# A hybrid decoder step on one core: the first norm's small products cut into pieces, operand differences emitted earlier, the first conv pair ordered by ready k, single PSUM banks placed first

## Chip, cores and metric

The kernel runs on one core of one Trainium2 chip. The metric is the device time of one execution in microseconds; where several executions were timed, the median stands. TensorE multiplies matrices into PSUM, VectorE and ScalarE do elementwise work and read PSUM, GpSimd does small copies, some sums and accumulating loads, and SyncE issues most loads.

## The reference, cut

One decoder layer works on 512 prompt tokens and 64 sample tokens with 1024 channels, in float32.

```python
xn = rms_norm(h, g_mix[i])
z = xn @ w_in[i]                       # 1024 x 6144: b, c, hc, v, two gates
ya, cb = gated_short_conv(b, c, hc, conv_bufs[i], w_conv[i])   # b * conv3(c * hc)
ya = ya @ w_out_conv[i]
yb, pb = multiscale_pool(v, pool_bufs[i], pos0, w_pool[i], pool_scale[i])
h = h + (gate_a * ya + gate_b * yb) @ w_o[i]
hn = rms_norm(h, g_mlp[i])
h = h + jnp.square(jax.nn.relu(hn @ w_up[i])) @ w_down[i]      # 1024 -> 4096 -> 1024
gp = jax.nn.sigmoid(rms_norm(h, g_ple[i]) @ w_ple_gate[i])
h = h + gp * (p[i] @ w_ple_proj[i])
return rms_norm(h, g_final), ...
```

## The kernel before

Channels lie on the 128 partitions, in NJ = 8 tiles; the 576 tokens lie on the free axis as NH = 2 halves of HT = 288 columns. Every float32 product is made of three products of a reduced type: each operand is split into `hi` (a cast on ScalarE, line 93 or 96) and `lo` (the remainder, on VectorE, line 94 or 97), and `mm` (line 104) issues hi x hi, hi x lo, lo x hi. A unit of 128 output channels over 8 k tiles and two halves is 48 such products; `product` (line 118) issues one. The input is scaled by the gain alone; the factor `r` of the norm is applied to the results.

Weights come through one stream (lines 180 to 247) in the order in which they are used. A load goes into one of eight raw slots, a split into one of seven slots (NF = 7); `take` splits ahead as far as these slots go, and with `live` it counts units that are still held. SyncE's queue issues the loads, GpSimd's queue those that add a second weight block to a loaded one.

Some matrix products are done as a two by two block scheme with seven block products (`pairs_of`, line 416). Its operands are blocks of the activations and differences of blocks: `Operand.differences` (line 407) makes three subtractions for each of four k pairs (lines 409, 411, 412) into a tile `gt` from a tile `gx`, and splits the four results, which are called `t1`, `t3` and `t2`, `t4`. The tiles `gx`, `gt` and the later `g` share two buffers under the tag "g". In `pairs_of`, `quarter` issues the 12 products of one block (four k pairs of three). With `late`, which before is set only for the first MLP block, the first four quarters leave their last k pair to the end, and five weights are held at once.

The opening runs so. The squares of the input are summed (`Rms.add`). Three first units (c, h and b of channel tile 0, in six single PSUM banks `ps0`) run over k in the outer loop (lines 486 to 488), 18 products for each k. After k = 5 `Rms.tokens` issues the norm's sums: 36 matmul instructions as the trace counts them, each with one moving column, followed by a root on ScalarE (line 333) and a chain of five small steps on VectorE that ends in `y` (line 340). After k = 6 `Rms.spread` brings `y` to all partitions (line 347), and `copies` makes `r` and its square `rs`. Then come channel tiles 0 and 4 of the conv branch (lines 554 to 569): the multiply of c by `rs` (line 558), the product with h, the convolution (line 526), the gate (line 538, first read of PSUM at line 542), and behind these the differences of two k pairs each. From line 571 on, three pairs of conv tiles and then the gates run through `pairs_of`.

Two things set the order. A planner takes the instructions in the order in which the program emits them, as priorities, and places on each engine the first one that it reckons to be ready by its own times; so an instruction can stand earlier than its line. From line 570 on (`pinned`), and again in the MLP, TensorE's products keep the program's order. Each engine then executes its own list in order.

PSUM has eight banks. The opening has one tile of two banks and six single ones, the middle part (lines 622 to 697) four tiles of two banks, the part from line 706 again one tile of two banks, allocated first, and six single ones (lines 707, 708), and the end four tiles of two. A new part's tile waits for the readers of the tiles that lay at its place. The middle part has 32 product tiles, which take the four places in turn; line 691 reads the last two. The part from line 706 opens with two units in four single banks (`two_products`, line 370).

Of the kernel before, what the change touches and what calls it, by code (L numbers as in the profile page):

```python
# [7 lines left out]
F32 = mybir.dt.float32  # L8
# [4 lines left out]
P = 128  # L13
D = 1024
NJ = D // P
# [3 lines left out]
NH = 2  # L19
HP = SEQ // NH  # L20
HB = DB // NH
HT = HP + HB * DS
# [12 lines left out]
G_MIX, W_CONV, P_SCALE, G_MLP, G_PLE, G_FINAL = 0, 1, 4, 5, 6, 7  # L35
NV = 8
KH = D // 2
NQ = NJ // 2
# [4 lines left out]
def tile_hybrid_step(ctx: ExitStack, tc: tile.TileContext, x, pt, vecs, rc, ident, sconv, spool, w_first, w_in,  # L43
                     w_pool, w_oc, w_o, w_up, w_down, w_pg, w_pp,
                     y_out, ncp, npp, ncs, nps):
    nc = tc.nc
# [10 lines left out]
    def pool(name, bufs, **kw):  # L57
        return scope.enter_context(tc.tile_pool(name=name, bufs=bufs, reuse_waits="tile", **kw))

    tmp, acts2 = pool("tmpx", 4), pool("acts1", 10)  # L60
    psum = pool("psumx", 1, space=bass.MemoryType.PSUM)
# [42 lines left out]
    def mm(outs, w, c, m, act, start, stop):  # L104

        wh, wl = (t[:, c % KH:c % KH + m] for t in w[c // KH])
        for i, (wt, at) in enumerate(((wh, act[0]), (wh, act[1]), (wl, act[0]))):
            for o, cols in outs:
                matmul(o, wt, cols(at), start=start and i == 0, stop=stop and i == 2)

    def both(ps):
        return [(ps[h] if isinstance(ps, list) else ps[:, h, :HT], lambda t, h=h: t[:, h, :]) for h in range(NH)]
# [5 lines left out]
    def product(unit, operands, base=0, m=P, step=P):  # L118

        ps = psum.tile([P, NH, 512], F32, tag="ps", name="ps") if banks is None else [bank() for _ in range(NH)]  # L120
        n = len(operands)
        steps(ps, unit, operands, range(n), base, m, step, 0, n - 1)
        return ps
# [129 lines left out]
    def v(i, j):  # L253
        return vec[:, i, j:j + 1]
# [47 lines left out]

    class Rms:
        def __init__(self, n=NH, width=HT, chunk=HT // 3):
            self.n, self.width, self.chunk, self.parts = n, width, chunk, []
            self.shape = [P, n, width]
            self.at = [(h, c) for h in range(n) for c in range(0, width, chunk)]

# [10 lines left out]
            else:  # L319
                nc.gpsimd.tensor_tensor(out=self.parts[0], in0=self.parts[0], in1=sq, op=ALU.add)  # L320

        def tokens(self, pin=False):

            n, m = len(self.at), self.chunk
            self.ps = ps = psum.tile([P, NH, 512], F32, tag="ps", name="psn")
            sums = ps[:m, 0, self.width:self.width + n]
            for i, (h, c) in enumerate(self.at):
                for k, a in enumerate(self.parts):
                    nc.tensor.matmul(  # L329
                        sums[:, i:i + 1], a[:, h, c:c + m], ones32[:, 0:1],  # L330
                        start=k == 0, stop=k == len(self.parts) - 1)
            rt, ms, y, t = (tmp.tile([m, n], F32, tag=g, name=g, bufs=2) for g in ("rt", "ms", "ry", "rz"))
            i = nc.scalar.activation(rt, sums, AF.Sqrt, bias=epst[:m], scale=1.0 / D)
            if pin:
                tc.keep_in_program_order(i)
            nc.vector.tensor_scalar(out=ms, in0=sums, scalar1=1.0 / D, scalar2=EPS, op0=ALU.mult, op1=ALU.add)
            nc.vector.reciprocal(y, rt)
            nc.vector.tensor_tensor(out=t, in0=y, in1=y, op=ALU.mult)
            nc.vector.scalar_tensor_tensor(out=t, in0=t, scalar=-0.5, in1=ms, op0=ALU.mult, op1=ALU.mult)
            nc.vector.scalar_tensor_tensor(out=y, in0=t, scalar=1.5, in1=y, op0=ALU.add, op1=ALU.mult)  # L340
            self.y = y

        def spread(self):

            m = self.chunk
            for i, (h, c) in enumerate(self.at):
                nc.tensor.matmul(  # L347
                    self.ps[:, h, c:c + m], self.y[:, i:i + 1].broadcast_to([m, P]), idt[:m, :m],
                    start=True, stop=True)
            return self.ps[:, :self.n, :self.width]  # L350
# [132 lines left out]
    for j in range(NJ):  # L483
        stat.add(xs[j], part=j >= NJ - 2)
    ps0 = [[bank() for _ in range(NH)] for _ in range(3)]
    for k in range(NJ):
        for u in range(3):
            mm(both(ps0[u]), [first[k]], u * P, P, xg[k], k == 0, k == NJ - 1)
        if k == 5:
            stat.tokens()  # L490
        if k == 6:
            r1, r1s = stat.copies(stat.spread(), "r", "rs")

    ncp_t = tmp.tile([P, NJ, CW - 1], F32, tag="ncp", name="ncp_t", bufs=1)
    xo = Operand(10)
# [4 lines left out]
    class Conv:  # L500
# [37 lines left out]
        def gate(self, ps):  # L538
# [11 lines left out]
                op=ALU.mult)  # L550
            ya_in[self.j] = split_act(bt)

    ya_in = [None] * NJ
    for j in (0, NQ):
        ps_c = ps0[0] if j == 0 else product(stream.take(2), xg)
        c = tmp.tile([P, NH, HT], F32, tag="t", name="c")
        for h in range(NH):
            nc.vector.tensor_tensor(out=c[:, h], in0=ps_c[h], in1=r1s[:, h], op=ALU.mult)
        ps_h = ps0[1] if j == 0 else product(stream.take(2), xg)
        conv = Conv(j)  # L560
        for h in range(NH):
            conv.half(h, ps_h[h], c[:, h])
        conv.convolve()
        conv.gate(ps0[2] if j == 0 else product(stream.take(2), xg))
        for k in range(j // 2, j // 2 + 2):
            g = tmp.tile([P, 4, HT], F32, tag="g", name="gx", bufs=2)
            for i in range(2):
                nc.scalar.mul(g[:, 2 * i:2 * i + 2], xs[k + i * NQ], v(G_MIX, k + i * NQ))
            xo.differences(k, g)
    pinned = True  # L570
    for q in range(1, NQ):

        def corner(i, g, c11):
            if i == 0:
                conv.lo = tmp.tile([P, NH, HT], F32, tag="t", name="c")
                nc.vector.tensor_tensor(out=conv.lo[:, 1], in0=c11, in1=r1s[:, 1], op=ALU.mult)
            else:
                conv.now.half(1, c11, conv.lo[:, 1])

        def finish(i, g):  # L580
            if i == 0:
                nc.vector.tensor_tensor(out=conv.lo[:, 0], in0=g[:, 0], in1=r1s[:, 0], op=ALU.mult)
                conv.hi = tmp.tile([P, NH, HT], F32, tag="t", name="c")
                nc.vector.tensor_tensor(out=conv.hi, in0=g[:, 2:4], in1=r1s, op=ALU.mult)
                conv.now = Conv(q)
            else:
                conv.now.half(0, g[:, 0], conv.lo[:, 0])
                conv.now.convolve()
                conv.then = Conv(q + NQ)
                conv.then.whole(g[:, 2:4], conv.hi)  # L590
                conv.now.gate(conv.ps)
                conv.then.convolve()

        def filler():
            conv.ps = product(stream.take(2), xg)

        pairs_of(2, xo, corner, finish, filler=filler)
        conv.then.gate(product(stream.take(2), xg))


# [103 lines left out]
    for j in halved:  # L704
        nc.sync.dma_start(xs[j], x[:, j])
    tmp = pool("tmpm", 3)
    psum = pool("psumm", 1, space=bass.MemoryType.PSUM)
    banks = pool("banks", 6, space=bass.MemoryType.PSUM)
    acts2 = pool("acts2", 6)
    pinned = True  # L710

# [215 lines left out]
```

## Time and profile before

| | |
|---|---|
| median of 3 executions | 896.02 us (894.7 to 897.62) |
| profiled execution | 897.59 us |
| its span | 895.8 us |
| mean granted clock of TensorE | 0.988 |
| busy: TensorE, VectorE, ScalarE, GpSimd | 98%, 65%, 45%, 15% of the span |

TensorE is busy nearly all the time, and a busy row does not say at which clock. The views used below are the page's summary, the list of waits, the timelines of single engines (each row is a run of like instructions: start, time from the first start to the last end, engine, line, operation, tiles, count, and in brackets the idle time before it and what ended it), and tables of stretches with the granted clock.

### The profile page before, as it was taken

Reading aid. Unit: us, or ns where it says so; the run is one execution under the profiler, and the core shown is the slowest. Engines: PE = TensorE matmul, PEld = TensorE weight load, DVE = VectorE, ACT = ScalarE, POOL = GpSimd, SP = SyncE. Lnnn points to the kernel's source line nnn. Section 1 sums busy time; section 2 is a strip of 40 time slices with the busy share of each in tenths; the row PEclk is TensorE's granted clock in tenths of the full one; section 3 lists DMA queues with packets and bytes.
Section 4 is the critical chain, followed back from the end, with each engine's and each line's share of the span. In section 5 each row is a group of like instructions: output and inputs, shape, how many; then the busy total and the mean of one; then the engine's idle time right before and its main releaser. Section 6 shows DMA issues by size and latency. Waiting matters only on the chain.

```text
span 895.8 us, 16709 instructions
## 1 busy us (share of the span) xinstructions
PE 878.8 (98%) x6554; PEld 875.5 (98%) x6554; DVE 581.2 (65%) x1027; ACT 405.0 (45%) x702; POOL 131.1 (15%) x168
## 2 busy tenths in 40 slices
PE   9989999999999999999999999999999999999995
PEld 9979999999999999999999999999999999999995
DVE  7886887985336677767884347534773367687455
ACT  7643443553113333345774237522672157536432
POOL 4101111100001221022110100011000110021354
PEclk9889999999999999999999999999999999999998
DMA  7526455554222222363553535353543544332002
GB/s 258 133 81 145 140 128 149 139 147 140 83 83 83 83 83 83 114 194 92 134 155 104 133 97 137 121 130 101 154 133 87 124 122 130 104 97 94 14 16 91
DMA packets 58125, 103.88 MB, mean 116 GB/s; under 512 B 6848, under 2 KB 10560, under 8 KB 58048
## 3 DMA queue, kind: packets, MB, share of 16 engines
q1 hardware_dynamic: 50416, 89.16, 31.0%
q0 software_dynamic: 7488, 13.63, 9.7%
q8 instruction: 51, 0.84, 0.4%
q14 instruction: 26, 0.21, 0.1%
q10 hardware_dynamic: 144, 0.03, 0.0%
HBM read 99.82 MB, written 2.99 MB: 115 GB/s over the span
## 4 chain that ended last, share of the span: by engine, by line
PE 94%; DVE 3%; DMA 1%; ACT 1%; issue 1%; SPq 0%; DVEq 0%
PE b L67 68%; PE ps L67 18%; PE psg L67 6%; DVE lo L94 1%; PE psn L329 1%; PE psn L347 1%; DMA raw<-w_up 1%; DMA xin<-x 0%; ACT hi L93 0%; DVE xall L808 0%; DVE t L691 0%; DVE gt L409 0%; ACT hi L96 0%; DVE gt L412 0%; DVE gt L411 0%
## 5 line engine op out<-in xcount | busy, mean ns | idle before, releaser
L67 PE MATMUL b<-hi 128*128 128x288 f32 x1592 | 403.1, 298 | 5.2 <-ACT hi L93 3.6
L67 PE MATMUL b<-lo,hi 128*128 128x288 f32 x1592 | 402.1, 297 | 0.7 <-DVE lo L94 0.7
L67 PE MATMUL b<-hi,lo 128*128 128x288 f32 x1592 | 402.1, 297 | 0.4 <-DVE lo L94 0.4
L93 ACT CAST hi<-raw 128x512 fp32r<-128x512 f32 x300 | 184.6, 620 | 323.6 <-PE b L67 214.6
L67 PEld LDWEIGHTS b<-hi 128*128 128x128 f32 x1592 | 278.0, 190 | 6.8 <-ACT hi L93 4.3
L94 DVE TENSOR_TENSOR lo<-raw,hi 128x512 fp32r<-128x512 f32 x300 | 210.6, 707 | 112.0 <-ACT hi L93 108.9
L67 PEld LDWEIGHTS b<-lo,hi 128*128 128x128 f32 x1592 | 278.1, 190 | 1.3 <-DVE lo L94 1.2
L67 PEld LDWEIGHTS b<-hi,lo 128*128 128x128 f32 x1592 | 277.7, 190 | 0.7 <-DVE lo L94 0.7
L67 PE MATMUL ps<-hi 128*128 128x288 f32 x416 | 89.2, 296 | 0.0
L67 PE MATMUL ps<-hi,lo 128*128 128x288 f32 x416 | 89.1, 296 | 0.0
L67 PE MATMUL ps<-lo,hi 128*128 128x288 f32 x416 | 89.1, 296 | 0.0
L154 POOL DMA_DIRECT2D raw<-w_up x32 | 27.7, 865 | 327.6 <-DMA raw<-w_up 188.8
L67 PEld LDWEIGHTS ps<-hi,lo 128*128 128x128 f32 x416 | 67.0, 189 | 0.0
L67 PEld LDWEIGHTS ps<-lo,hi 128*128 128x128 f32 x416 | 67.0, 189 | 0.0
L67 PEld LDWEIGHTS ps<-hi 128*128 128x128 f32 x416 | 67.0, 189 | 0.0
L320 POOL TENSOR_TENSOR sq<-sq 128x576 f32<-128x576 f32 (+2 forms) x32 | 41.2, 1286 | 112.3 <-ACT sq L314 64.6
L174 DVE TENSOR_TENSOR s<-raw 128x512 f32<-128x512 f32 x26 | 17.9, 690 | 49.3 <-DMA raw<-w_up 32.5
L93 ACT CAST hi<-s 128x512 fp32r<-128x512 f32 x52 | 32.0, 617 | 38.1 <-PE b L67 33.0
L94 DVE TENSOR_TENSOR lo<-s,hi 128x512 fp32r<-128x512 f32 x52 | 35.7, 687 | 13.1 <-ACT hi L93 12.1
L67 PE MATMUL psg<-hi 128*128 128x320 f32 (+1 forms) x128 | 38.2, 298 | 0.7 <-ACT r L354 0.7
L67 PE MATMUL psg<-lo,hi 128*128 128x320 f32 (+1 forms) x128 | 37.9, 296 | 0.0
L67 PE MATMUL psg<-hi,lo 128*128 128x320 f32 (+1 forms) x128 | 37.9, 296 | 0.0
(130 smaller groups left out, 751.0 us busy)
## 6 DMA issues: line engine op xcount, KB each, us to landing
raw<-w_in SPq DMA_DIRECT2D x100, 256.0 KB, 2.9
raw<-w_up SPq DMA_DIRECT2D x80, 256.0 KB, 2.9
raw<-w_down SPq DMA_DIRECT2D x64, 256.0 KB, 2.9
raw<-w_up POOLq DMA_DIRECT2D x32, 256.0 KB, 4.4
raw<-w_in POOLq DMA_DIRECT2D x20, 256.0 KB, 4.9
raw<-w_oc SPq DMA_DIRECT2D x16, 256.0 KB, 2.8
raw<-w_o SPq DMA_DIRECT2D x16, 256.0 KB, 2.8
raw<-w_pg SPq DMA_DIRECT2D x16, 256.0 KB, 2.8
```

The source lines that it names most:

```text
L67: i = nc.tensor.matmul(*args, **kw)
L93: nc.scalar.copy(hi, src)
L94: nc.vector.tensor_tensor(out=lo, in0=src, in1=as32(hi), op=ALU.subtract)
L154: nc.gpsimd.dma_start(raw, y, accum_op=ALU.add)
L174: nc.vector.tensor_tensor(out=p.rs2, in0=p.rs1, in1=p.ra, op=ALU.add)
L320: nc.gpsimd.tensor_tensor(out=self.parts[0], in0=self.parts[0], in1=sq, op=ALU.add)
L329: nc.tensor.matmul(sums[:, i:i + 1], a[:, h, c:c + m], ones32[:, 0:1], start=k == 0, stop=k == len(self.parts) - 1)
L347: nc.tensor.matmul(self.ps[:, h, c:c + m], self.y[:, i:i + 1].broadcast_to([m, P]), idt[:m, :m], start=True, stop=True)
```

## The change

The norm's sums become a function of their own, `sums`, which can be called with some of the six pieces of the tokens, and `spread` can be called likewise. At k = 5 the sums of two pieces follow each of the three units' six products. Then the last two k run unit by unit; the spread of three pieces stands after k = 6 of the second unit and that of the other three after k = 7.

The differences of k pairs 0 and 2 are emitted before the convolution of their tile, those of 1 and 3 before its gate and behind the third unit's product. The first conv pair (q = 1) runs `pairs_of` with `late`. In the part from line 706 the six single banks are allocated ahead of the tile of two banks.

```diff
--- before.py
+++ after.py
@@ -302,7 +302,7 @@
 
     class Rms:
         def __init__(self, n=NH, width=HT, chunk=HT // 3):
-            self.n, self.width, self.chunk, self.parts = n, width, chunk, []
+            self.n, self.width, self.chunk, self.parts, self.ps = n, width, chunk, [], None
             self.shape = [P, n, width]
             self.at = [(h, c) for h in range(n) for c in range(0, width, chunk)]
 
@@ -319,16 +319,25 @@
             else:
                 nc.gpsimd.tensor_tensor(out=self.parts[0], in0=self.parts[0], in1=sq, op=ALU.add)
 
-        def tokens(self, pin=False):
+        def sums(self, pieces):
 
             n, m = len(self.at), self.chunk
-            self.ps = ps = psum.tile([P, NH, 512], F32, tag="ps", name="psn")
-            sums = ps[:m, 0, self.width:self.width + n]
-            for i, (h, c) in enumerate(self.at):
+            if not self.ps:
+                self.ps = psum.tile([P, NH, 512], F32, tag="ps", name="psn")
+            sums = self.ps[:m, 0, self.width:self.width + n]
+            for i in pieces:
+                h, c = self.at[i]
                 for k, a in enumerate(self.parts):
                     nc.tensor.matmul(
                         sums[:, i:i + 1], a[:, h, c:c + m], ones32[:, 0:1],
                         start=k == 0, stop=k == len(self.parts) - 1)
+
+        def tokens(self, pin=False, summed=False):
+
+            n, m = len(self.at), self.chunk
+            if not summed:
+                self.sums(range(n))
+            sums = self.ps[:m, 0, self.width:self.width + n]
             rt, ms, y, t = (tmp.tile([m, n], F32, tag=g, name=g, bufs=2) for g in ("rt", "ms", "ry", "rz"))
             i = nc.scalar.activation(rt, sums, AF.Sqrt, bias=epst[:m], scale=1.0 / D)
             if pin:
@@ -340,10 +349,12 @@
             nc.vector.scalar_tensor_tensor(out=y, in0=t, scalar=1.5, in1=y, op0=ALU.add, op1=ALU.mult)
             self.y = y
 
-        def spread(self):
+        def spread(self, pieces=None):
 
             m = self.chunk
             for i, (h, c) in enumerate(self.at):
+                if pieces is not None and i not in pieces:
+                    continue
                 nc.tensor.matmul(
                     self.ps[:, h, c:c + m], self.y[:, i:i + 1].broadcast_to([m, P]), idt[:m, :m],
                     start=True, stop=True)
@@ -483,13 +494,21 @@
     for j in range(NJ):
         stat.add(xs[j], part=j >= NJ - 2)
     ps0 = [[bank() for _ in range(NH)] for _ in range(3)]
-    for k in range(NJ):
+    def first_step(k, u):
+        mm(both(ps0[u]), [first[k]], u * P, P, xg[k], k == 0, k == NJ - 1)
+
+    for k in range(NJ - 2):
         for u in range(3):
-            mm(both(ps0[u]), [first[k]], u * P, P, xg[k], k == 0, k == NJ - 1)
-        if k == 5:
-            stat.tokens()
-        if k == 6:
-            r1, r1s = stat.copies(stat.spread(), "r", "rs")
+            first_step(k, u)
+            if k == NJ - 3:
+                stat.sums((2 * u, 2 * u + 1))
+    stat.tokens(summed=True)
+    for u in range(3):
+        for k in (NJ - 2, NJ - 1):
+            first_step(k, u)
+            if u == 1:
+                r = stat.spread(range(3 * (k - NJ + 2), 3 * (k - NJ + 3)))
+    r1, r1s = stat.copies(r, "r", "rs")
 
     ncp_t = tmp.tile([P, NJ, CW - 1], F32, tag="ncp", name="ncp_t", bufs=1)
     xo = Operand(10)
@@ -550,6 +569,12 @@
                 op=ALU.mult)
             ya_in[self.j] = split_act(bt)
 
+    def differences(k):
+        g = tmp.tile([P, 4, HT], F32, tag="g", name="gx", bufs=2)
+        for i in range(2):
+            nc.scalar.mul(g[:, 2 * i:2 * i + 2], xs[k + i * NQ], v(G_MIX, k + i * NQ))
+        xo.differences(k, g)
+
     ya_in = [None] * NJ
     for j in (0, NQ):
         ps_c = ps0[0] if j == 0 else product(stream.take(2), xg)
@@ -560,13 +585,11 @@
         conv = Conv(j)
         for h in range(NH):
             conv.half(h, ps_h[h], c[:, h])
+        differences(j // 2)
         conv.convolve()
-        conv.gate(ps0[2] if j == 0 else product(stream.take(2), xg))
-        for k in range(j // 2, j // 2 + 2):
-            g = tmp.tile([P, 4, HT], F32, tag="g", name="gx", bufs=2)
-            for i in range(2):
-                nc.scalar.mul(g[:, 2 * i:2 * i + 2], xs[k + i * NQ], v(G_MIX, k + i * NQ))
-            xo.differences(k, g)
+        ps_b = ps0[2] if j == 0 else product(stream.take(2), xg)
+        differences(j // 2 + 1)
+        conv.gate(ps_b)
     pinned = True
     for q in range(1, NQ):
 
@@ -594,7 +617,7 @@
         def filler():
             conv.ps = product(stream.take(2), xg)
 
-        pairs_of(2, xo, corner, finish, filler=filler)
+        pairs_of(2, xo, corner, finish, q == 1, filler=filler)
         conv.then.gate(product(stream.take(2), xg))
 
 
@@ -704,8 +727,8 @@
     for j in halved:
         nc.sync.dma_start(xs[j], x[:, j])
     tmp = pool("tmpm", 3)
+    banks = pool("banks", 6, space=bass.MemoryType.PSUM)
     psum = pool("psumm", 1, space=bass.MemoryType.PSUM)
-    banks = pool("banks", 6, space=bass.MemoryType.PSUM)
     acts2 = pool("acts2", 6)
     pinned = True
```

## Rows read from the trace of the kernel before

**Rows 1.** The page's part 1: TensorE's busy time, share of the span, instructions.

```profile
PE 878.8 (98%) x6554; PEld 875.5 (98%) x6554; DVE 581.2 (65%) x1027; ACT 405.0 (45%) x702; POOL 131.1 (15%) x168
```

**Rows 2.** Waits of TensorE, whole span: line, waited for, us in total, times, longest.

```profile
PE b L67 <- ACT hi L93: 3.6, 3, 1.9
...
PE b L67 <- DVE t L691: 1.0, 1, 1.0
...
PE psg L67 <- ACT r L354: 0.7, 1, 0.7
```

**Rows 3.** Timeline of TensorE, first norm.

```profile
21.03 0.42 PE L67 MATMUL b<-lo,hi 128*128 128x288 f32 x2
21.29 0.43 PE L67 MATMUL b<-hi,lo 128*128 128x288 f32 x2
21.56 3.55 PE L329 MATMUL psn<-ones,sq 128*96 128x1 f32 x36
24.97 0.83 PE L67 MATMUL b<-hi 128*128 128x288 f32 x2
...
30.64 1.62 PE L347 MATMUL psn<-idt,ry 96*128 96x96 f32 x12
```

**Rows 4.** Stretches: length, TensorE busy, granted clock, DMA share and GB/s.

```profile
24.00:24.50 0.50, 0.50 (x7) 0.61 0.60 148
30.80:31.00 0.20, 0.20 (x4) 0.66 1.20 225
58.00:59.00 1.00, 0.00 (x0) 0.62 0.00 0
65.00:66.00 1.00, 1.00 (x9) 0.97 0.00 0
454.00:455.00 1.00, 1.00 (x14) 1.00 0.67 236
```

**Rows 5.** Timeline of VectorE, behind the first norm.

```profile
27.31 0.15 DVE L340 SCALAR_TENSOR_TENSOR ry<-rz,ry 96x6 f32<-96x6 f32 x1
...
33.58 0.82 DVE L558 TENSOR_TENSOR c<-b,rs 128x288 f32<-128x288 f32 x2 [2.94 <-ACT rs L358]
```

**Rows 6.** Timeline of TensorE, opening of the first conv pair.

```profile
55.20 0.29 PE L67 MATMUL b<-hi,lo 128*128 128x288 f32 x1
56.49 0.40 PE L67 MATMUL b<-hi 128*128 128x288 f32 x1 [1.00 <-ACT hi L93]
...
59.86 0.61 PE L67 MATMUL b<-hi 128*128 128x288 f32 x1 [1.95 <-ACT hi L93]
...
65.11 0.30 PE L67 MATMUL b<-lo,hi 128*128 128x288 f32 x1
```

**Rows 7.** Timeline of VectorE, operands of the first conv pair.

```profile
48.23 0.45 DVE L412 TENSOR_TENSOR gt<-gx,gt 128x288 f32<-128x288 f32 x1
...
53.00 0.82 DVE L542 TENSOR_TENSOR bt<-b,r 128x288 f32<-128x288 f32 x2 [0.89 <-PE b L67]
...
57.36 0.76 DVE L409 TENSOR_TENSOR gt<-gx 128x576 f32<-128x576 f32 x1
...
59.02 1.58 DVE L94 TENSOR_TENSOR lo<-gt,hi 128x576 fp32r<-128x576 f32 x2
```

**Rows 8.** Timeline of ScalarE, casts there.

```profile
55.19 0.67 ACT L93 CAST hi<-bt 128x576 fp32r<-128x576 f32 x1
55.77 0.67 ACT L93 CAST hi<-gt 128x576 fp32r<-128x576 f32 x1
```

**Rows 9.** Timeline of TensorE, second MLP block and the second norm's sums.

```profile
449.75 0.37 PE L67 MATMUL b<-hi 128*128 128x288 f32 x1 [0.46 <-DVE g L443]
...
452.25 0.37 PE L67 MATMUL b<-hi 128*128 128x288 f32 x1 [0.66 <-ACT hi L93]
...
453.91 1.10 PE L329 MATMUL psn<-ones,sq 128*96 128x1 f32 x12
```

**Rows 10.** Timeline of VectorE, second MLP block.

```profile
445.22 0.69 DVE L174 TENSOR_TENSOR s<-raw 128x512 f32<-128x512 f32 x1 [2.57 <-DMA raw<-w_up]
```

## The prediction

> **What bounds the kernel now.** I read the page first: TensorE is busy 98% of the span [rows 1], and the chain that ended last is almost all TensorE. So what can be saved is the time in which TensorE stands still or runs at its lower clock. The view of TensorE's waits gives the first kind: the largest entry is 3.6 us for operand casts in three waits, then 1.0 us for a read of PSUM by VectorE at line 691 and 0.7 us for a ScalarE copy at line 354 [rows 2]. The stretches by granted clock give the second kind: within the first 70 us the clock falls twice, near 24 us and near 58 us, and comes back near 31 us and 65 us [rows 4]. It is 1.00 elsewhere until the last few us. The four parts of the change lie at just these places, so I price each there.
>
> **Part 1, the norm's small products.** Before, 36 products with one moving column start at 21.56 and hold TensorE until 24.97 [rows 3], that is 95 ns each. During them the clock falls to the lower level, 1.2 of 2.4 GHz (0.61 is the mean of the half microsecond in which it falls) [rows 4]. From 24.97 to 30.64 TensorE issues 23 large products: 5.67 us, or 247 ns each. At full clock a pair of them starts 0.26 us after the pair before (21.03 and 21.29 [rows 3]), 0.1325 us each by the exact steps around them, so 23 take 3.05 us. The lower clock costs 5.67 - 3.05 = 2.6 us here. The change removes no product: 36 stay at 95 ns, as three pieces of 12 (1.1 us) with six large products (0.8 us) between them. So it gains 2.6 us if the clock holds and nothing if it does not. For holding: later norms issue 12 such products in a row (453.91 [rows 9]) with the clock at 1.00 [rows 4], and a piece has the size of such a run. Against: three pieces come within 5 us, which no row shows. The bounds are a gain of 2.6 and a loss of about 0.5 (the fall coming some large products earlier); I take 2.6, because each single piece is as long as the run at 453.91.
>
> The Trainium skill, "TensorE: Matmul & The Clock Gate", section "Why this matters for your kernels", asks for no idle gaps between bursts of matmuls to keep the clock. Here TensorE issued back to back and the clock still fell, so the rule by itself does not explain the row; taken literally it would let the pieces change nothing, and the sum would be 2.6 us higher.
>
> The norm's two other steps move too. The spread needs the factor `y`, whose last step starts on VectorE at 27.31 and takes 0.15 [rows 5], 2.5 us after the sums. The emission has 18 large products between sums and spread as before; the planner put 23 there, because in its own reckoning `y` was late, and I expect about 23 again: 3.05 us at full clock, so `y` is in time by 0.5 us. After the spread 13 large products remained before; now 12 or 13 remain, 1.6 us. The spread's end to the first multiply with `rs` took about 1.5 us (32.1, by the 1.62 us from 30.64 less the pipelined overlap [rows 3], to 33.58 [rows 5]) and this multiply frees the first two banks for the next unit 0.5 us later, so a wait of 0.3 to 0.5 us stays at this place, at most 0.2 us longer than now. I charge **0.2**.
>
> **Parts 2 and 3, the opening of the first conv pair.** From 55.20 to 65.11 [rows 6] TensorE starts 23 products in 9.91 us, where 3.05 would do: the loss is **6.9 us**. Two long gaps (1.00 and 1.95 us [rows 6]) are waits for casts of operand differences, two short ones make 0.7, and 17 products after 61 us run at the lower clock that the gaps brought on (about 17 x 0.108 = 1.8 us). The reason is on VectorE and ScalarE. The third subtraction for k = 2 is made at 48.23 [rows 7], but its cast comes only at 55.77, right behind the cast of the gated conv product at 55.19 [rows 8], and that one waits for TensorE's third unit, through line 542 at 53.00, which itself follows 0.89 us of VectorE idle [rows 7]. Only then do the subtractions for k = 3 run (57.36), and its last casts' remainders end at 59.02 + 1.58 = 60.60 [rows 7]. With two buffers under the tag "g" the k = 3 tile cannot start before the k = 2 tile is fully cast, so one late cast delays everything.
>
> The change emits k = 2 ahead of the convolution and k = 3 ahead of the gate. What stood in front goes behind: the gate's 53.00 to 55.77, and the idle 0.89, together 3.7 us. So k = 3 is complete at about 60.60 - 3.7 = 56.9, and its first half, about 1.5 us sooner, at 55.4; k = 2 is cast soon after 48.7, about 50 to 51. TensorE enters the pair at 52.9. With the ready k pairs first it has 36 products, 4.8 us, before it touches k = 3: it needs the second half of k = 2 at 54.9, `t3` of k = 3 at 58.1, `t2` of k = 3 at 60.5. Each is there 2 to 4 us sooner. So I expect no wait in the opening and no fall of the clock: the gain is the whole 6.9. The gate moves 3 us later on VectorE; who waits for it is the fifth bank of the pair, needed only at 60.9, and the output projection, 150 us later. No DMA is issued by the differences, and GpSimd's small copies of the convolution go behind them at no cost that the chain sees.
>
> The order by ready k has its own price. It holds five of the seven split weight slots, so the weights of the next blocks, their SP loads and the accumulating GpSimd loads behind them come later. The MLP does the same in its first pair: there the first block shows no wait, but in the next one VectorE waits 2.57 us for such a load [rows 10] and TensorE 0.46 and 0.66 us behind it [rows 9]. So the price lies between 0 and 1.1; I take **0.4**, since here no row shows the loads late before the change.
>
> **Part 4, single banks first.** The opened output units need four banks. With the two-bank tile placed first, those are banks 2 to 5, among them the third of the four earlier tiles. Thirty-two product tiles rotate over four slots, so the last two products lie in the third and fourth slot, and line 691 reads the third for 1.0 us while TensorE waits [rows 2]. Placed from bank 0, the opened units reuse the slots of the gate products, which were read long before. Their operands are ready: 72 products (9.5 us) come before the last two k. Gain 1.0. At the end of the MLP the first two-bank tile then no longer lies over the norm's spread, which ScalarE copies at line 354, but over banks whose copies came earlier; the first gated product needs the copy only after its 24 products. Gain 0.7. Both are TensorE time on the chain, and it has no wait behind either that would take the time back. Bounds 0 and 1.7; I take **1.7**, as the code fixes the places.
>
> **The sum.** 2.6 + 6.9 + 1.7 = 11.2 gained, 0.2 + 0.4 paid: 10.6 us off the profiled execution's 897.59 (span 895.8 and 1.8 around it), so **887.0**. That execution stands 1.6 above the median of 896.02; taken from the median the sum is 885.4, and I count this into the low end, since the runs may differ in where the clock comes back.
>
> **The rivals.**
> A second fall (B): the clock falls during the three pieces as it does now. For it: the same 36 products lie within 5 us. Against: no 36 stand in a row. 887.0 + 2.6 = **889.6**. This is also what the page's rule on gaps gives by itself.
> The operands stay late (C): the planner, which places an instruction when it reckons it ready, leaves the k = 2 cast at 55.77. Then only the order by k helps: `t2` of k = 2 is complete near 57.3 instead of 54.9, a wait of 2.4 us, and k = 3 is hidden behind the 36 products. 887.0 + 2.4 = **889.4**; with B, **892.0**.
> Nothing but the banks (D): the planner restores the old order on all engines; only 1.7 is gained, **895.9**.
> Slower (E): the weight slots. The lag that the first pair leaves in the stream may not be caught up; each of the ten blocks up to the end of the gates (two in each of three conv pairs, four gates) then loses 1.1 us as the MLP's second block does [rows 9, 10], 11 us, and with the second fall 889.6 + 11 = **900.6**. It decides only if about seven blocks or more lose so much. Against it: in the MLP only one block loses after the first pair, and TensorE has no wait for weights between 66 and 370 us now.
>
> **How the numbers follow.** A difference under 0.3% (2.7 us) cannot be told from no change here. The forecast has 0.48, B 0.20, C 0.16, B with C 0.06, D 0.05, E 0.05. A, B and C are all faster by over 0.3%: 0.90. D is within: 0.05; E is slower: 0.05. The range goes from 884.0 (the sum from the median, the late order free and a little of spread) to 892.0 (B with C), which leaves out D, E and some tails, about 2 in 10.
>
> **What would show it.** Right: the granted clock at 1.00 from 20 to 70 us; the sums as three groups of 12; no wait of TensorE for a cast in the pair's opening; the k = 3 subtractions on VectorE ahead of line 542's counterpart for the second unit; no wait for lines 691 and 354. Wrong: a stretch of large products at 240 ns after the sums (B); a cast of k = 2 behind that of the gate (C); long waits for raw weights on VectorE in the conv pairs, with waits of TensorE behind them (E).

## The result and the profile after

The changed kernel takes 888.36 us in the median of six executions (886.44 to 891.53), against 897.19 us before in the same setting: ratio 0.9908, 95% interval 0.9886 to 0.9930. Four further executions on another chip gave 886.81 us, ratio 0.9888 (0.9872 to 0.9903). By the two intervals it is faster by 6 to 11.5 us. The profiled execution is the fastest of the first six, 886.44 us with a span of 884.7, 11.1 us below the span before; that of the kernel before (897.59 us) lies at the slow end of its executions, so the two traces lie further apart than the medians (8.8 and 9.6 us). The ratios compare executions in the usual state alone; one of the twelve of part 1 alone, below, ran at a mean clock of 0.844 in 946.86 us and is left out.

The page of the changed kernel: span, busy time and instructions of the engines, and TensorE's granted clock in tenths, 40 slices.

```profile
span 884.7 us, 16702 instructions
...
PE 873.0 (99%) x6554; PEld 870.4 (98%) x6554; DVE 581.2 (66%) x1027; ACT 404.8 (46%) x702; POOL 132.1 (15%) x168
...
PEclk9999999999999999999999999999999999999998
```

The clock has no low slice before the last one; before, the second and third slice were 8, for the two falls in [rows 4]. TensorE's waits in the changed kernel (waited for; us in total, times, longest), without those at the two ends of the program:

```profile
PE b L67 <- ACT hi L93: 0.7, 1, 0.7
...
PE b L67 <- DVE lo L94: 0.4, 1, 0.4
PE b L67 <- DVE g L454: 0.3, 1, 0.3
PE b L67 <- DVE c L583: 0.2, 1, 0.2
```

The waits for casts in the opening of the conv pair, for line 691 (1.0) and for line 354 (0.7) [rows 2] are gone. What stands here is small and lies elsewhere.

The norm in the changed kernel, timeline of TensorE, answering [rows 3]:

```profile
19.94 1.10 PE L331 MATMUL psn<-ones,sq 128*96 128x1 f32 x12
...
21.78 1.10 PE L331 MATMUL psn<-ones,sq 128*96 128x1 f32 x12
...
23.63 1.10 PE L331 MATMUL psn<-ones,sq 128*96 128x1 f32 x12
24.59 0.52 PE L67 MATMUL b<-hi 128*128 128x288 f32 x2
...
27.73 0.81 PE L358 MATMUL psn<-idt,ry 96*128 96x96 f32 x6
...
28.53 0.81 PE L358 MATMUL psn<-idt,ry 96*128 96x96 f32 x6
...
31.17 0.40 PE L67 MATMUL b<-hi 128*128 128x288 f32 x1 [0.21 <-DVE c L583]
```

Three groups of 12 sums, six large products between them; from 24.59 on 23 large products again (the planner kept its 23), then the spread in two halves with one product between, and at 31.17 a wait of 0.21 for the multiply with `rs`. Stretches of the changed kernel (length, TensorE busy, granted clock, DMA share and GB/s):

```profile
20.00:31.00 11.00, 10.96 (x97) 1.00 0.75 182
48.00:62.00 14.00, 13.92 (x103) 1.00 0.28 93
...
438.00:444.00 6.00, 5.02 (x38) 1.00 0.57 139
```

The clock is 1.00 over the norm and over the opening of the pair, and TensorE is busy 13.92 of 14 us there. VectorE and ScalarE in the opening, answering [rows 7] and [rows 8]; line 420 is the first subtraction (409 before), 423 the third (412), 561 the gate's read (542):

```profile
48.79 0.74 DVE L420 TENSOR_TENSOR gt<-gx 128x576 f32<-128x576 f32 x1
...
51.10 0.44 DVE L423 TENSOR_TENSOR gt<-gx,gt 128x288 f32<-128x288 f32 x1
51.47 0.81 DVE L561 TENSOR_TENSOR bt<-b,r 128x288 f32<-128x288 f32 x2
52.28 0.76 DVE L94 TENSOR_TENSOR lo<-gt,hi 128x576 fp32r<-128x576 f32 x1
```

```profile
51.57 0.68 ACT L93 CAST hi<-gt 128x576 fp32r<-128x576 f32 x1 [0.56 <-DVE gt L423]
53.81 0.68 ACT L93 CAST hi<-bt 128x576 fp32r<-128x576 f32 x1 [1.56 <-DVE bt L565]
```

The k = 3 subtractions start at 48.79, ahead of the gate's read at 51.47, and the last remainder ends at 53.04. The cast of the gate's product (53.81) now stands behind all operand casts. The two bank places, first the opening of the output projection, then the first gated product behind the last spread:

```profile
366.53 0.43 PE L67 MATMUL ps<-hi,lo 128*128 128x288 f32 x2
366.80 0.42 PE L67 MATMUL b<-hi 128*128 128x288 f32 x2
```

```profile
819.02 1.48 PE L358 MATMUL psn<-idt,ry 96*128 96x96 f32 x12
820.28 0.40 PE L67 MATMUL psg<-hi 128*128 128x320 f32 x1
```

At both places TensorE goes on without a wait.

**Where the time went, stretch by stretch.** To compare traces I cut each at five events of the timelines: the first multiply with `rs` on VectorE (the norm's end), the first product into the four two-bank tiles, the first product into the single banks of the later part, the last pair of residual adds of the output projection on VectorE (its start), and the first gated product. Behind the last event come 64 to 65 us more, which the table leaves out. The table gives the length of the stretches between them in us; the first column is counted from the span's start. It holds for all the traces that follow.

| kernel (one trace each) | norm | conv, gates | output conv, pool | output projection | MLP |
|---|---|---|---|---|---|
| before | 33.58 | 175.67 | 167.53 | 51.37 | 403.27 |
| changed | 30.66 | 169.76 | 166.38 | 51.26 | 402.22 |
| changed, again | 32.20 | 169.76 | 166.39 | 52.58 | 402.29 |
| part 1 alone | 30.46 | 175.68 | 167.53 | 52.15 | 403.20 |
| part 2 alone (differences sooner) | 31.84 | 169.25 | 167.53 | 51.80 | 403.28 |
| part 3 alone (ready k) | 30.50 | 172.16 | 167.54 | 51.58 | 403.16 |
| part 4 alone (banks) | 33.55 | 175.67 | 166.38 | 51.74 | 402.27 |
| changed without part 1 | 31.60 | 169.33 | 166.38 | 51.26 | 402.29 |
| changed without part 3 | 30.50 | 169.24 | 166.39 | 51.26 | 402.39 |
| changed without part 3, again | 30.54 | 169.24 | 166.38 | 51.26 | 402.19 |
| parts 2 and 4 | 30.05 | 169.25 | 166.38 | 51.26 | 402.32 |
| changed without part 3, six pieces | 30.93 | 168.82 | 166.38 | 51.67 | 402.30 |
| changed without part 3, six slots | 32.28 | 169.24 | 166.39 | 51.26 | 400.82 |
| changed, 24 sums | 32.35 | 171.28 | 166.38 | 52.83 | 402.37 |

The columns of conv, pool and MLP fall into levels that mostly repeat within 0.2 us (with 24 sums the conv stretch holds a wait and a fall of the clock); the norm and the output projection vary from execution to execution. Between the traces of the first two rows, 2.92 come from the norm, 5.91 from the conv stretch, 1.15 from the bank place before the projection, 0.1 from the projection and 1.05 from the MLP and the bank place at its end: 11.1 in all.

### The profile page after: what moved, and what is told of

Read it like the earlier page. It is cut to its first block, busy times and chain, and to the rows that moved or that the text cites. A ratio compares the mean times of both kernels' runs of the same rounds, so it can differ in the third digit from the quotient of the medians.

```text
span 884.7 us, 16702 instructions
## 1 busy us (share of the span) xinstructions
PE 873.0 (99%) x6554; PEld 870.4 (98%) x6554; DVE 581.2 (66%) x1027; ACT 404.8 (46%) x702; POOL 132.1 (15%) x168
## 4 chain that ended last, share of the span: by engine, by line
PE 95%; DVE 2%; DMA 1%; ACT 1%; issue 1%; SPq 0%; DVEq 0%
PE b L67 69%; PE ps L67 19%; PE psg L67 6%; DVE lo L94 1%; PE psn L331 1%; PE psn L358 1%; DMA raw<-w_up 1%; DMA xin<-x 0%; DVE xall L831 0%; ACT hi L93 0%; ACT hi L96 0%; ACT sq L314 0%; DVE g L454 0%; DVE u L452 0%; DVE s L174 0%
## 5 line engine op out<-in xcount | busy, mean ns | idle before, releaser
L93 ACT CAST hi<-s 128x512 fp32r<-128x512 f32 x52 | 32.0, 618 | 38.0 <-PE b L67 33.4
```

The costliest lines, as they stand in the source:

```text
L93: nc.scalar.copy(hi, src)
```

## The experiments

**Each part alone.** Four kernels, each the kernel before with one part, on one chip.

Part 1, the sums in pieces:

```diff
+    for k in range(NJ - 2):
         for u in range(3):
+            first_step(k, u)
+            if k == NJ - 3:
+                stat.sums((2 * u, 2 * u + 1))
+    stat.tokens(summed=True)
...
```

> The kernel before with part 1 alone: the norm's sums in three pieces of 12 between groups of six large products. Theory (pieces hold the clock): granted clock 1.00 from 20 to 31 us, and 2 to 2.6 us less than before, in the median and in every execution. Rival (the clock falls in part of the executions all the same): the span is 2 to 3 us shorter in some and equal in others, with mean clock near 0.988 where equal; median gain 0 to 2. The two long waits of the conv pair's opening stay in both, 6.9 us.

Measured: ratio 0.9992 (0.9983 to 1.0), so 0 to 1.5 us less than before. Stretches of its trace:

```profile
20.00:31.00 11.00, 10.79 (x95) 1.00 0.71 183
...
428.00:432.00 4.00, 2.60 (x15) 1.00 0.45 108
```

In the traced execution the clock holds over the norm (1.00) and the norm ends 3.1 us earlier than before (30.46 against 33.58). But TensorE is busy only 2.60 of 4 us at the opening of the MLP, a stretch in which the kernel before had no wait, so 0.8 of it is paid back there (output projection 52.15 against 51.37). The mean clocks of the other executions (0.990 to 0.993) hardly stand above those of before (0.987 to 0.993). The rival, that the clock falls in part of the executions all the same, is the nearer one.

Part 2, the differences emitted sooner:

```diff
             conv.half(h, ps_h[h], c[:, h])
+        differences(j // 2)
         conv.convolve()
-        conv.gate(ps0[2] if j == 0 else product(stream.take(2), xg))
+        ps_b = ps0[2] if j == 0 else product(stream.take(2), xg)
+        differences(j // 2 + 1)
+        conv.gate(ps_b)
```

> The kernel before with the differences emitted sooner alone, without the order by ready k. Theory of the prediction (both are needed): the k = 3 operands come about as the pair first asks for them, so a wait of 0 to 1.5 us is left and 5.5 to 6.9 us are gained. Rival (the cast order alone was the cause): no wait of TensorE for a cast between 52 and 62 us, the clock stays at 1.00 there, gain 6.9 us. Other rival (the order by k carries the gain): gain under 3 us.

Measured: ratio 0.9937 (0.9925 to 0.9949), 890.84 us against 896.47. Its stretches:

```profile
24.00:28.00 4.00, 4.00 (x23) 0.57 0.72 147
50.00:62.00 12.00, 12.00 (x92) 1.00 0.28 96
```

No wait is left: 12.00 of 12 us busy at clock 1.00 from 50 to 62 us. The conv stretch is 6.42 us shorter, and that with the pair still in its old order. So the place of the cast was the cause; the first row shows the norm's fall, which this kernel still has. The pair's first product and the last remainder for k = 3, from the timelines of TensorE and VectorE:

```profile
51.65 0.30 PE L67 MATMUL b<-hi 128*128 128x288 f32 x1
53.47 0.76 DVE L94 TENSOR_TENSOR lo<-gt,hi 128x576 fp32r<-128x576 f32 x1
```

The remainder ends at 54.23, 2.6 us behind the pair's first product. The old order reaches the products of `t2` with k = 3 after 21 others, 2.8 us (21 x 0.1325): the operand is there just in time.

Part 3, the order by ready k:

```diff
-        pairs_of(2, xo, corner, finish, filler=filler)
+        pairs_of(2, xo, corner, finish, q == 1, filler=filler)
```

> The kernel before with the order by ready k alone, the differences where they were. By the prediction's case C: the second half of the k = 2 operands is complete near 57.3 us instead of 54.9, one wait of about 2.4 us, the k = 3 operands hidden behind the 36 products of the ready k; gain 4.5 us if the clock holds, 2.5 to 3 if the wait makes it fall. Rival (with late operands the order by k only moves the waits): gain under 1 us.

Measured: ratio 0.9956 (0.9941 to 0.9972), 893.3 us. Timeline of TensorE in its opening, the two waits:

```profile
53.84 0.40 PE L67 MATMUL b<-hi 128*128 128x288 f32 x1 [1.40 <-ACT hi L93]
54.73 0.40 PE L67 MATMUL b<-lo,hi 128*128 128x288 f32 x1 [0.49 <-DVE lo L94]
```

With the operands late as before, the order by k turns 6.9 us of loss into two waits of 1.40 and 0.49 us, and the clock stays up. The conv stretch is 3.51 us shorter, between the expected 4.5 and the rival's less than 1. The traced execution is the fastest of seven (890.6 us); the mean clocks of the others go down to 0.991, so the clock need not have stayed up in all of them.

Part 4, the banks:

```diff
+    banks = pool("banks", 6, space=bass.MemoryType.PSUM)
     psum = pool("psumm", 1, space=bass.MemoryType.PSUM)
-    banks = pool("banks", 6, space=bass.MemoryType.PSUM)
```

> The kernel before with the six single banks placed first, alone. Theory: the waits for lines 691 and 354 are gone, TensorE goes on at once at both places, gain 1.7 us. Rival (another reader of the banks or an operand comes next): a new wait of 0.5 to 1 us at one of the places, gain 0 to 1 us.

Measured: ratio 0.9972 (0.9962 to 0.9983), 1.5 to 3.4 us. In its trace the pool stretch is 1.15 and the MLP 1.00 shorter, with no new wait at either place: 2.15 in all.

**What each part is worth beside the others.** Four kernels on a second chip.

> The changed kernel itself once more, on another chip, for the spread of its executions. Theory now (the pieces hold the clock in some executions only): mean clocks between 0.991 and 0.997, the spans of the low ones 2 to 4 us longer; in a trace of a low one large products at about 240 ns right behind the sums. Rival (the spread comes from waits elsewhere): all traces and mean clocks without a fall in the norm.

Measured: 886.81 us, mean clocks 0.992, 0.996, 0.996, 0.996. The traced execution was the one at 0.992 (889.98 us). Its stretches:

```profile
24.00:25.00 1.00, 1.00 (x12) 0.98 0.68 240
25.00:28.00 3.00, 3.00 (x14) 0.50 0.64 111
28.00:29.00 1.00, 1.00 (x8) 0.81 0.75 125
424.00:428.00 4.00, 3.04 (x21) 1.00 0.47 89
```

Here the clock falls near 25 us and comes back in the 29th, with the sums in pieces: the norm ends at 32.20 instead of 30.66. And at 424 to 428 the opening of the MLP loses a microsecond more. It is the same program with the same lists of every engine. Of the 3.5 us between the two spans, 1.5 lie in the norm, 1.3 in the output projection and 0.6 behind the last event of the table; the spread of the other executions (886 to 891) may have the same places, but they were not traced.

The changed kernel without part 1:

```diff
-            if k == NJ - 3:
-                stat.sums((2 * u, 2 * u + 1))
...
+        if k == 5:
+            stat.tokens()
```

> The changed kernel with the norm's sums in one run again. If part 1 is worth what it showed alone: 0.3 to 1.5 us slower than the changed kernel in the median, mean clock never above 0.995. By the prediction: 2.6 us slower. Rival (part 1 does nothing): equal, and the same mean clocks.

Measured: 887.47 us (ratio 0.9897, 0.9882 to 0.9911), 0.7 above the changed kernel, with intervals that overlap, and mean clocks of 0.993 to 0.995. Its norm, with one run of 36 sums:

```profile
23.00:24.00 1.00, 1.00 (x15) 0.98 0.71 225
24.00:27.00 3.00, 3.00 (x15) 0.50 0.65 150
27.00:28.00 1.00, 1.00 (x8) 0.81 0.94 113
```

The fall is half as long as the one in the trace of before: about 3.4 us at the low clock instead of 6.8 [rows 4].

The changed kernel without part 3 (the short diff above, reversed):

> The changed kernel without the order by ready k. By the differences-alone run, where no wait for an operand was left in the opening: within 0.7 us of the changed kernel, either way, and no wait of TensorE for a cast between 48 and 60 us. Rival (with TensorE some 2.5 us earlier the k = 3 operands come too late without it): one wait of 0.5 to 2 us in the opening, 0.5 to 3 us slower.

Measured: 885.99 us (ratio 0.9881, 0.9867 to 0.9894), 0.8 under the changed kernel, the intervals overlap. No wait in the opening: the conv stretch is 169.24, against 169.76 with the order by k. So on top of part 2 the order gains nothing, and costs 0.5 us. Timeline of TensorE's weight loads in the changed kernel, where these lie:

```profile
56.66 0.19 PEld L67 LDWEIGHTS b<-hi 128*128 128x128 f32 x1 [0.31 <-ACT g L432]
...
60.44 0.19 PEld L67 LDWEIGHTS b<-hi 128*128 128x128 f32 x1 [0.16 <-DVE g L454]
```

TensorE waits for ScalarE's copy out of the first bank (line 432), since only six products now stand between that bank's last product and the next ones that add to it, and for VectorE's sum of line 454. The kernel without part 3 has neither wait.

One square more on GpSimd, 24 sums instead of 36:

```diff
-    stat.add(xs[j], part=j >= NJ - 2)
+    stat.add(xs[j], part=j >= NJ - 1)
```

> The changed kernel with one more square added on GpSimd, so that the sums are 24 products instead of 36, in pieces of 8, each six large products later than before. 12 products of 95 ns fewer: 1.1 us less, and the clock holds in more executions (mean clock 0.995 and above), another 1 us in the median. Rival (the GpSimd sum comes late): a wait of 0.5 to 1.5 us for it ahead of the sums, or for the spread behind them, equal or slower.

Measured: 890.37 us (ratio 0.9927, 0.9913 to 0.9942), 3.6 slower than the changed kernel. Timeline of TensorE behind its sums:

```profile
29.45 1.58 PE L358 MATMUL psn<-idt,ry 96*128 96x96 f32 x12 [1.37 <-DVE ry L349]
...
32.86 0.40 PE L67 MATMUL b<-hi 128*128 128x288 f32 x1 [1.40 <-DVE c L585]
```

The sums are shorter, but they come six products later, and TensorE then waits 1.37 us for `y` and 1.40 us for the multiply with `rs`: the rival. Behind these waits the clock falls as well, at 33.4 us. The large products that stand between sums and spread are needed as cover for VectorE's chain.

**What is left over.** Four kernels on a third chip; the first is the changed kernel without part 3, as a reference.

> The changed kernel without the order by ready k once more, for a reference on the same chip as the next three. 885.5 to 888: where the clock falls in the norm 1.5 to 3 us over the fastest, and up to 1.4 us where the second load behind line 174 lands late.

Measured: 885.78 us (ratio 0.9877, 0.9861 to 0.9893), mean clocks 0.995 and 0.996.

> The differences sooner and the banks first, with the norm's sums in one run and without the order by ready k. If part 1 only makes the fall of the clock rarer: 0.5 to 1.5 us over the kernel with the pieces in the median, its fastest execution within 0.7 us of the other's fastest. By the prediction's size for part 1: 2.6 us over it.

This kernel has the diffs of parts 2 and 4 only. Measured: 885.80 us (ratio 0.9878, 0.9862 to 0.9894), mean clocks 0.995 and 0.996. Its stretches and its norm on TensorE:

```profile
20.00:31.00 11.00, 10.91 (x97) 1.00 0.71 171
48.00:62.00 14.00, 14.00 (x108) 1.00 0.31 105
```

```profile
21.13 3.14 PE L329 MATMUL psn<-ones,sq 128*96 128x1 f32 x36
```

One run of 36 sums, and the clock stays at 1.00. The median equals that of the kernel with the pieces on the same chip (885.78). The whole gain of the changed kernel, within the intervals, comes from parts 2 and 4.

Six pieces of six sums between groups of three large products:

```diff
-            if k == NJ - 3:
-                stat.sums((2 * u, 2 * u + 1))
+            for h in range(NH):
+                first_step(k, u, h)
+                stat.sums((2 * u + h,))
```

> As the reference, with the sums in six pieces of six products between groups of three large ones, over the same stretch. If the fall depends on how long a run of small products is: no fall in any execution, mean clock 0.995 to 0.997 throughout, 0 to 1 us faster in the median. If it depends on how many small products lie in the whole stretch: the same mean clocks and the same median as with three pieces.

Measured: 886.06 us (ratio 0.9877, 0.9858 to 0.9896), mean clocks 0.996 and 0.997. It does not tell the two readings apart, since on this chip neither the traces nor the mean clocks show a fall in the reference, or with one run of 36.

One slot fewer for split weights:

```diff
-NF = 7
+NF = 6
```

> As the reference, with six slots for split weights instead of seven, so that a weight is split one unit later and line 174 comes later in VectorE's order. If VectorE standing at line 174 behind an accumulating load is what makes the MLP's opening late in some executions: the wait there falls under 1 us, the last output unit's sum always 51.3 us after the output projection's opening, 0 to 1 us faster in the median. Rival (less lookahead costs more than it saves): new waits of TensorE for casts or remainders of weights, 1 to 6 us slower.

Measured: 886.61 us in the median (ratio 0.9878, 0.9858 to 0.9899), its fastest execution 884.09, the lowest of all. First two rows of VectorE, the first two weight sums of the MLP, then stretches of TensorE:

```profile
389.08 0.69 DVE L174 TENSOR_TENSOR s<-raw 128x512 f32<-128x512 f32 x1 [0.65 <-DMA raw<-w_up]
...
401.88 0.68 DVE L174 TENSOR_TENSOR s<-raw 128x512 f32<-128x512 f32 x1
```

```profile
25.00:29.00 4.00, 4.00 (x21) 0.57 0.73 156
...
438.00:444.00 6.00, 6.00 (x51) 1.00 0.63 144
```

The wait at line 174 is 0.65 us at the first of these sums and none at the second, the one at which every other kernel here waits 2.6 to 4.6 us. The projection takes 51.26, as expected (five traces with seven slots have this too), and the MLP is 1.4 us shorter than in any other kernel, with TensorE busy throughout 438 to 444 where the changed kernel has 5.02 of 6. Against that stands a fall of the clock in the norm in its trace (0.57 over 25 to 29), and mean clocks of 0.992 and 0.993 in three of four executions. Whether six slots make the fall more frequent is open, so this is no clear gain in the median.

## Why the prediction held, and where its terms were off

The time, 888.36 us, lies 1.4 above the forecast 887.0 and inside the range; the direction and about the size were right. The closeness is in part luck. The traces of before and after differ by 11.1, near the forecast 10.6, but the fall in the norm stands in the first of them alone; the medians differ by 8.8 and 9.6. Part 1 was counted about 2 us too high, parts 2 and 3 half a microsecond to one too high, part 4 half a microsecond too low, and the sum started 0.4 above the median (897.59 against 897.19). Term by term:

**Parts 2 and 3, 6.9 forecast.** The mechanism was right: the cast behind the gate's product delayed the k = 2 tile, that one the k = 3 tile, and behind the idle time the clock fell; it did so in all three traces that have these four waits, and in no trace of the pair's opening without them. Measured in the conv stretch: 5.91 with both parts, 6.42 with the differences alone, 3.51 with the order by k alone. The step that failed is the need for the order by k. I let TensorE ask for `t2` of k = 3 only at 60.5 and counted on that cover, because I put the operand's end at 56.9, 4.0 us behind the pair's opening at 52.9. With part 2 alone it ends 2.6 us behind the opening, and the old order asks at 2.8. The 0.4 charged to the order by k came out at 0.5 (169.76 against 169.24), but by luck: I had charged it to the weight slots, and no wait for weights shows. The two waits for line 432 and line 454, which I had not counted, make it up. The wait of 0.2 charged to the norm is the one at 31.17; it lies in this stretch too.

**Part 1, 2.6 forecast.** This term was mis-sized: 0 to 1.5 alone, 0.7 in the full kernel, nothing beside parts 2 and 4 alone, though the two traces compared first show 2.92. The step that failed is taking the fall in one execution as the kernel's own. Of six traces with one run of 36, two fall for about 6.8 us (before, part 4 alone), two for about 3.4 (part 2 alone, changed without part 1), and two not at all (part 3 alone, parts 2 and 4). Of seven with pieces, two fall for about 3.4 us and five hold. So the pieces may make the fall rarer and shorter, but these counts are too few to show it, and a fall is not excluded by them, which was my rival B. It was no alternative to the forecast, as I had put it: both happen, in different executions of one program. What decides between them in an execution is not settled.

The Trainium skill's page "TensorE: Matmul & The Clock Gate" says, under "What's actually happening", that the same kernel issues a different number of matmuls at the low clock from run to run; it speaks of the start of a kernel. The two traces of the changed kernel show such a difference in the middle of the work: no fall in one, a fall near 25 us in the other. The Trainium skill's rule on idle gaps (same page, "Why this matters for your kernels"), which I weighed before, leaves the pieces without effect; the medians agree with that within their intervals, but the fall without any gap remains outside it.

Two small numbers belong to this term. At full clock 36 sums in a row take 3.14 us from first start to last end, against 3.55 before, so I was wrong to hold their price fixed: the fall also slowed the sums. And from the first sum to the multiply with `rs` the pieces take 10.72 us with 12 large products more among them (12 x 0.1325 = 1.59), 9.13 without these; with one run and no fall it is 8.92 (21.13 to 30.05). The pieces thus cost 0.2 us by themselves.

**Part 4, 1.7 forecast.** 1.15 and 1.00 in the stretches, 2.15 together, 1.5 to 3.4 in the median. The places were right, both a little under-sized (1.0 and 0.7 forecast).

**What I had not counted.** The opening of the MLP. VectorE stands at line 174 for a weight sum of the MLP whose second half GpSimd's accumulating load brings, while the residual adds of the projection wait behind it. The row of VectorE in the first trace of the changed kernel, then in the second, and TensorE in the second:

```profile
396.47 0.69 DVE L174 TENSOR_TENSOR s<-raw 128x512 f32<-128x512 f32 x1 [2.59 <-DMA raw<-w_up]
```

```profile
399.93 0.69 DVE L174 TENSOR_TENSOR s<-raw 128x512 f32<-128x512 f32 x1 [4.50 <-DMA raw<-w_up]
```

```profile
425.52 0.40 PE L67 MATMUL b<-lo,hi 128*128 128x288 f32 x1 [0.51 <-DVE lo L94]
...
426.89 0.40 PE L67 MATMUL b<-hi 128*128 128x288 f32 x1 [0.45 <-ACT g L432]
```

The wait is 2.59 us in one and 4.50 in the other. With the longer one the last residual add comes late, and TensorE has to wait for a remainder and a copy at the pair's opening: 51.26 and 52.58 us for the projection. The other traces with seven slots fall into roughly the same order: a wait up to 2.7 us goes with 51.26 us, 3.1 with 51.37, 3.5 to 3.7 with 51.6 to 51.8, and 4.3 to 4.6 (24 sums; part 1 alone, which paid back part of its gain here) with 52.83 and 52.15. The kernel with six slots, where the second sum of line 174 comes later in VectorE's list, has no wait there and the short projection, as this reading asks. That it also shortens the MLP by 1.4 was not forecast; the two waits that I named for the order by k in the MLP [rows 9] are the ones that went. In the changed kernel they are still there:

```profile
439.55 0.37 PE L67 MATMUL b<-hi 128*128 128x288 f32 x1 [0.31 <-DVE g L454]
...
442.05 0.37 PE L67 MATMUL b<-hi 128*128 128x288 f32 x1 [0.67 <-ACT hi L93]
```

The rivals: C (operands stay late) did not occur, and part 3 alone showed its price, 2 waits of together 1.9 us where I had worked out 2.4. D and E did not occur; TensorE has no waits for weights in the conv pairs.

## What to carry to other kernels

Where an engine with a list in order waits for a late operand, look at what stands in front of its producer on the other engines' lists: moving the emission of the early operands ahead of work that waits for TensorE was worth 6.4 us, and reordering the consumer added nothing once that was done. A loss to the clock read from one execution is that execution's: look at the mean clocks of several before it enters a sum. The kernels with the shortest medians here have parts 2 and 4, without the order by k (885.8 to 886.0 us, with or without the pieces); on one chip the one with the pieces lies 0.8 us under the changed kernel, which the intervals do not separate.

## What the runs showed of the hardware

The clock of TensorE fell behind a run of small products without any idle time, in one traced execution and not in the other of the same program; where it fell in the norm, the low stretch lasted about 6.8 us in two traces and about 3.4 us in four. In the kernel with 24 sums it fell only at 33 us, behind two waits of TensorE. An accumulating load of 256 KB issued by GpSimd landed 3.9 us after its issue in one execution and 5.6 us in another (issued at 392.55 and 394.31, line 174 at 396.47 and 399.93), and VectorE, whose list has that sum next, stood idle for 2.59 and 4.50 us until then.
